# Encoder with a PEER mixer on one core: two more up-projection blocks ahead of the first gate loads, the one-hots of the gate matrix built four steps ahead and gated on GpSimd

## The chip, the core and the metric

One core of one Trainium2 chip runs the whole program as one launch. The metric is the device time of that launch in microseconds (us), lower is better. Three runs of the kernel before took 3058.64 to 3060.64 us, median 3059.3 us.

## What is computed

One encoder layer on 512 tokens of width 2048: windowed attention beside a bidirectional recurrent block, an output projection, and a PEER channel mixer. The change lies in the PEER mixer. Its reference, cut:

```
q = (xt @ w_pq).reshape(T, PEER_HEADS, 2, PEER_HALF)
s1, s2 = einsum(q[:, :, 0], sub_k1), einsum(q[:, :, 1], sub_k2)
v1, i1 = lax.top_k(s1, 16);  v2, i2 = lax.top_k(s2, 16)
cand = v1[..., :, None] + v2[..., None, :]
sc, sel = lax.top_k(cand, 16)          # per head; expert = i1 * 128 + i2
gates = softmax(sc)
act = gelu(einsum('cd,ced->ce', xc, u_emb[expert]))
out = einsum('ce,ced->cd', gates * act, v_emb[expert])
```

There are 16384 experts, 128 of them per token (8 heads of 16).

## The kernel before

Attention, the recurrence, the output projection and the PEER queries fill the first 880 us or so. From there on the program works through the experts.

**Two ways to the experts.** Tokens 0 to 159 gather the rows of their experts from HBM (`gather_gen`): a gather is an indirect DMA that GpSimd (POOL) issues (L1147), and each is followed by one VectorE (DVE) instruction over 2048 elements, a product with the token's row (`gu`, L1154) or a weighted sum (`gv`, L1173). One such pair is a tick. Two gathers are always issued ahead. The other 352 tokens are computed densely: all experts, in 128 blocks of 128, with weights that are zero where a token did not choose an expert.

**The dense part.** An up-projection block (`u_block`) multiplies one block of u_emb with the 352 tokens: 48 matmuls on TensorE (PE), L297 to L299. Its float32 weights are loaded by SyncE (SP, L255) and split into a rounded part `hi` (ScalarE, ACT, L269) and a rest `lo` (DVE, L281). `take` for block b issues the split of block b+1. ACT applies the gelu (L1123, `ga`), and the result stays in SBUF or is spilled to HBM (`ad`).

**The gate matrix.** The weights of the dense tokens form a matrix G (expert by token), made by `g_step`, 4 tokens at a time, in 88 steps. For each token a one-hot row of i1 (`ohA`) and of i2 (`ohB`) is made on DVE (L1208, two instructions of 512 elements a step). `ohA` is multiplied by the gate: in even steps on DVE (L1214, one instruction), in odd steps on ACT (L1212, four). Four small matmuls (L1234, `ps_G`) make 4 columns of G, ACT copies them to a staging tile (L1219), and after 32 tokens the tile goes to HBM (`gd`, L1221). `g_onehots(n + 3)` is called in step n.

**The order.** `stage_plan` writes the order of this stage by hand before the program is built. It walks through the blocks with assumed costs for PE, DVE and ACT and fills hooks, four in each u block (after every 12 matmuls), with the routing work, the gate steps and the ticks. Blocks with hooks come first (here 37, blocks 0 to 36); three more u blocks follow (37 to 39), and together they are `lead0` = 40. All engines take their instructions in this order.

**The transition.** After block 36 the staging tiles are written out, and SP is asked for G tiles (`load_g`, L1315, waiting for `gd`) and for spilled activations (`reload`, L1310, `gr`). Blocks 37 to 39 each call `beside`, which runs due ticks and `weigh` for 3 expert blocks: DVE multiplies by G (L1321), ACT rounds the product (L1324, `Wh`), DVE takes the rest (L1325, `Wl`). After block 39 the down-projection units (`v_unit`, L1368 to L1370) and the remaining u blocks alternate until about 2960 us.

Of the kernel before, what the change touches and what calls it, by code (L numbers as in the profile page):

```python
# [8 lines left out]
F32 = mybir.dt.float32  # L9
# [3 lines left out]
AF = mybir.ActivationFunctionType  # L13
ALU = mybir.AluOpType
# [28 lines left out]
NB = 4  # L43
G_AHEAD = 3
G_STEPS = [(tt, t) for tt in range(1, NT) for t in range(NB1 if tt == 1 else 0, 128, NB)]

# [11 lines left out]
def stage_plan():  # L58
# [8 lines left out]
    for r in range(6):  # L67
# [3 lines left out]
        if r < 5:  # L71
# [5 lines left out]
                      ("lists", 2)]}.get(r, [])  # L77
    tasks += [("pre", m) for m in range(G_AHEAD)]
    for n in range(len(G_STEPS)):
# [5 lines left out]
    while tasks:  # L85
# [4 lines left out]
        while tasks and max(dve, act) <= pe:  # L90
            if ticks_on and since >= 3.5:
                cur.append(("tick", None))
                dve, since = dve + 2.35, 0.0
                continue
            t = tasks.pop(0)
            if t[0] == "g":
                cost, arg = ((1.37, 2.2, 1.22), (2.06, 0.6, 1.22))[t[1] % 2], t[1]
            elif t[0] == "pre":
                cost, arg = ((2.06, 0.0, 0.0), (1.37, 1.6, 0.0))[t[1] % 2], t[1]
            elif t[0] == "lists":  # L100
                cost, arg = (0.0, 0.5, 0.9), t[1]
            elif t[0] in ("soft_a", "soft_b"):
                cost, arg = (t[2], 0.5, 0.0), t[1]
            else:
                cost, arg = t[1:], None
            cur.append((t[0], arg))
            dve, act, pe = dve + cost[0], act + cost[1], pe + cost[2]
            if t[0] == "prime":
                ticks_on, since = True, -9.0
            if ticks_on:  # L110
                since += cost[0]
            if t[0] in ("tr", "soft_a", "lists"):
                break
# [3 lines left out]
    hooks += [[] for _ in range(4 * nbg - len(hooks))]  # L117
    lead0 = nbg + 3
    done, runs, order = lead0, [], [("u", b) for b in range(lead0)]
# [27 lines left out]
def tile_encoder(  # L147
# [1052 lines left out]
    As, Bs, evac, gst = {}, {}, [], {}  # L1200

    def g_onehots(n):
        tm, ta = G_STEPS[n]
        lt = lts[tm]
        Bs[n] = B = gst["oh"].tile([128, NB, 128], F32, tag="B", name="ohB", bufs=G_AHEAD + 1)
        As[n] = Ao = gst["oh"].tile([128, NB, 128], F32, tag="A", name="ohA", bufs=G_AHEAD + 1)
        for o, j in ((Ao, 0), (B, 1)):
            V.tensor_tensor(o, io_sb.unsqueeze(1).to_broadcast([128, NB, 128]),  # L1208
                            lt[:, j, ta:ta + NB].unsqueeze(2).to_broadcast([128, NB, 128]), op=ALU.is_equal)
        if n % 2:  # L1210
            for t in range(NB):
                A.activation(out=Ao[:, t, :], in_=Ao[:, t, :], func=AF.Copy, scale=lt[:, 2, ta + t:ta + t + 1])  # L1212
        else:
            V.tensor_tensor(Ao, Ao, lt[:, 2, ta:ta + NB].unsqueeze(2).to_broadcast([128, NB, 128]), op=ALU.mult)  # L1214

# [7 lines left out]
    def g_step(n):  # L1223
        flush_evac()
        if n + G_AHEAD < len(G_STEPS):
            g_onehots(n + G_AHEAD)
        tt, ta = G_STEPS[n]
# [54 lines left out]
    psS[:] = [psA, "A"]  # L1282
    for b in range(lead0 - 3):
        hk = iter(hooks[4 * b:4 * b + 4])
# [46 lines left out]

    due = {"now": 0.0, "per": (2 * (NSLOT + NB1) - ticks["n"]) / (2 * NBLK - PR - lead0 + 3)}

# [17 lines left out]

    load_g(0)
    load_g(1)
    for _ in range(3):
        reload()
    for i in range(3):
        u_block(lead0 - 3 + i, beside=lambda: beside(range((0, 3, 6)[i], (3, 6, PR + LEAD)[i])))

# [198 lines left out]
```

## Time and profile before

| what | value |
|---|---|
| median of three runs | 3059.3 us (3058.64 to 3060.64) |
| the profiled execution | 3060.12 us, its span 3058.3 us |
| PE busy in the span | 2933.6 us (96%), clock 0.986 of full |
| DVE busy | 2272.5 us (74%) |
| ACT busy | 1153.3 us (38%) |
| POOL busy | 846.3 us (28%) |
| gate stage, blocks 15 to 36 | 1014.9 to 1293.8 us |

The span is the profile's stretch from the first to the last instruction; the execution takes 1.8 us more. Busy shares are means over stages: in the stretch from 2000 to 2800 us PE is busy for 799.68 of 800 us, so there it sets the pace, while around the gate stage it waits for other engines. In the timeline an instruction's row gives start, duration, engine, line, operation, output and input tiles, and in brackets the idle time of the engine before it and what ended it.

### The profile page before, as it was taken

The page shows a single profiled execution, that of the slowest core. Times are in us where ns is not written, and L with a number is a line of the kernel's source. Part 1 is how long each engine was busy: PE and PEld are TensorE (multiplying, and loading weights), DVE is VectorE, ACT ScalarE, POOL GpSimd, SP SyncE. Part 2 cuts the span into 40 slices and gives each one's busy share as a digit, 9 for nine tenths or more (in the row PEclk, how much of TensorE's full clock was granted, in tenths as well). Part 3 has the DMA queues.
Part 4 walks back from the last instruction along what each step waited for, and adds up shares of the span by engine and source line. Part 5 has one row for each costly group of instructions (what it writes and reads, how often), then busy time and mean ns, then how long its engine had stood idle before and what let it go on. Part 6 is the DMA issues. An engine that isn't in the chain of part 4 may idle for free. (4 is left out here: it accounts for less than half of the span.)

```text
span 3058.3 us, 41550 instructions
## 1 busy us (share of the span) xinstructions
PE 2933.6 (96%) x16965; PEld 2729.7 (89%) x16965; DVE 2272.5 (74%) x3143; ACT 1153.3 (38%) x1529; POOL 846.3 (28%) x539
## 2 busy tenths in 40 slices
PE   8999989999999989979999999999999999999997
PEld 6777867788889988979999999999999999999996
DVE  5773367444987789857888888888787887888874
ACT  5663244343444455523322232323323233232233
POOL 0000121022545113423323433233232333233312
PEclk9999999999999999989999999999999999999998
DMA  5222220133225777789899998988889898898983
GB/s 228 76 85 87 85 109 29 69 131 121 83 101 194 258 281 291 298 316 338 335 337 358 355 345 332 343 335 336 328 333 338 326 342 339 340 343 322 349 300 114
DMA packets 160623, 766.76 MB, mean 251 GB/s; under 512 B 13744, under 2 KB 72896, under 8 KB 74480
## 3 DMA queue, kind: packets, MB, share of 16 engines
q1 hardware_dynamic: 101712, 378.44, 33.8%
q0 software_dynamic: 48000, 345.73, 29.9%
q10 hardware_dynamic: 10720, 39.93, 3.4%
q8 instruction: 133, 2.18, 0.3%
q14 instruction: 58, 0.48, 0.0%
HBM read 722.42 MB, written 41.63 MB: 250 GB/s over the span
## 5 line engine op out<-in xcount | busy, mean ns | idle before, releaser
L281 DVE TENSOR_TENSOR lo<-raw,hi 128x2048 fp32r<-128x2048 f32 x307 | 708.5, 2308 | 456.2 <-ACT hi L269 454.0
L269 ACT CAST hi<-raw 128x2048 fp32r<-128x2048 f32 x316 | 602.4, 1907 | 764.5 <-PE ps_v L1369 517.1
L297 PE MATMUL ps_u<-H,hi 128*128 128x352 f32 x2048 | 666.8, 326 | 14.9 <-ACT hi L269 14.9
L299 PE MATMUL ps_u<-H,lo 128*128 128x352 f32 x2048 | 662.5, 323 | 14.3 <-DVE lo L281 14.3
L1368 PE MATMUL ps_v<-Wh,hi 128*128 128x352 f32 x2048 | 664.0, 324 | 6.8 <-ACT Wh L1324 6.2
L1370 PE MATMUL ps_v<-Wh,lo 128*128 128x352 f32 x2048 | 663.6, 324 | 7.2 <-DVE lo L281 7.2
L1369 PE MATMUL ps_v<-Wl,hi 128*128 128x352 f32 x2048 | 663.4, 324 | 0.8
L298 PE MATMUL ps_u<-L,hi 128*128 128x352 f32 x2048 | 661.3, 323 | 0.0
L1147 POOL DMA_INDIRECT gu<-in_u_emb_dram,idx x160 | 331.6, 2073 | 691.4 <-DVE x L1173 500.9
L1147 POOL DMA_INDIRECT gv<-in_v_emb_dram,idx x160 | 286.7, 1792 | 658.8 <-DVE gu L1154 466.1
L299 PEld LDWEIGHTS ps_u<-H,lo 128*128 128x128 f32 x2048 | 385.6, 188 | 17.7 <-DVE lo L281 17.7
L297 PEld LDWEIGHTS ps_u<-H,hi 128*128 128x128 f32 x2048 | 385.9, 188 | 15.4 <-ACT hi L269 15.2
L1368 PEld LDWEIGHTS ps_v<-Wh,hi 128*128 128x128 f32 x2048 | 386.7, 189 | 10.8 <-ACT Wh L1324 8.0
L1370 PEld LDWEIGHTS ps_v<-Wh,lo 128*128 128x128 f32 x2048 | 386.4, 189 | 8.3 <-DVE lo L281 8.3
L1369 PEld LDWEIGHTS ps_v<-Wl,hi 128*128 128x128 f32 x2048 | 386.5, 189 | 2.2 <-DVE Wl L1325 2.2
L298 PEld LDWEIGHTS ps_u<-L,hi 128*128 128x128 f32 x2048 | 385.9, 188 | 0.0
L1154 DVE SCALAR_TENSOR_TENSOR gu<-gu,xng 128x2048 f32<-128x2048 f32 x160 | 364.8, 2283 | 4.2 <-DMA gu<-in_u_emb_dram,idx 4.2
L1173 DVE SCALAR_TENSOR_TENSOR x<-gv,w,x 128x2048 f32<-128x2048 f32 x128 | 300.1, 2345 | 2.9 <-DMA gv<-in_v_emb_dram,idx 2.6
L1123 ACT ACTIVATE ga<-ps_u 128x352 f32<-128x352 f32 x128 | 59.1, 462 | 195.3 <-PE ps_u L299 194.3
L1324 ACT CAST Wh<-ga 128x352 fp32r<-128x352 f32 x73 | 35.5, 487 | 223.3 <-DVE ga L1321 223.3
L297 PE MATMUL ps_cm<-xh,hi 128*128 128x512 f32 x256 | 106.0, 414 | 11.5 <-ACT xh L369 9.1
L1234 PE MATMUL ps_G<-ohA,ohB 128*128 128x128 f32 x704 | 92.0, 279 | 25.4 <-ACT stg L1219 17.4
(311 smaller groups left out, 3792.3 us busy)
## 6 DMA issues: line engine op xcount, KB each, us to landing
raw<-in_u_t_dram SPq DMA_DIRECT2D x128, 1024.0 KB, 6.2
raw<-in_v_t_dram SPq DMA_DIRECT2D x128, 1024.0 KB, 9.0
raw<-in_w_dram SPq DMA_DIRECT2D x28, 1024.0 KB, 4.8
gd<-stg ACTq DMA_DIRECT2D x11, 2048.0 KB, 10.1
G<-gd SPq DMA_DIRECT2D x32, 704.0 KB, 11.0
raw<-in_w_out_dram SPq DMA_DIRECT2D x16, 1024.0 KB, 4.7
raw<-in_w_pq_dram SPq DMA_DIRECT2D x16, 1024.0 KB, 5.0
ad<-ga ACTq DMA_DIRECT2D x55, 176.0 KB, 3.5
```

Of the source, the lines that this page charges most:

```text
L269: A.copy(hi, raw)
L281: en.tensor_tensor(lo[:, c], raw[:, c], hi.bitcast(F32)[:, c], op=ALU.subtract)
L297: T.matmul(ps, ah, bh, start=first, stop=False)
L298: T.matmul(ps, ah, bl, start=False, stop=False)
L299: T.matmul(ps, al, bh, start=False, stop=last)
L1147: P.indirect_dma_start(out=g, out_offset=None, in_=u_emb if kind == "u" else v_emb, in_offset=bass.IndirectOffsetOnAxis(ap=ix, axis=0))
L1154: V.scalar_tensor_tensor(out=g, in0=g, scalar=1.0, in1=xs_t["x"], op0=ALU.mult, op1=ALU.mult, accum_out=a_t[h][:, k:k + 1])
L1173: V.scalar_tensor_tensor(out=d, in0=g, scalar=wk, in1=d, op0=ALU.mult, op1=ALU.add)
L1234: T.matmul(ps[:, t, :], B[:, t, :], Ao[:, t, :], start=True, stop=True)
L1368: T.matmul(ps[:, 0:TD], hi[:, cc], Wh, start=j == 0, stop=False)
L1369: T.matmul(ps[:, 0:TD], hi[:, cc], Wl, start=False, stop=False)
L1370: T.matmul(ps[:, 0:TD], lo[:, cc], Wh, start=False, stop=j == PR - 1)
```

## The change

Four things change together.

1. The planner books both kinds of gate step at the same cost and allows a hook to end after an odd step. It now fills 33 blocks with hooks where it filled 37.
2. The multiplication of `ohA` by the gate leaves DVE and ACT and goes to POOL, one instruction of 128x512 for every step (88 in all).
3. `g_onehots` is split: in step n, `ohA` of step n + 4 and `ohB` and the multiplication of step n + 3 are issued. `ohA` has five buffers, `ohB` four.
4. `N_TRANS` = 5 u blocks stand between the last hook block and the first `v_unit`, and the G tiles and spilled activations are requested after the second. So `lead0` is 38, and 52 blocks are spilled where 55 were.

```diff
+N_TRANS = 5
-    tasks += [("pre", m) for m in range(G_AHEAD)]
+    tasks += [("pre", m) for m in range(G_AHEAD + 1)]
...
-                cost, arg = ((1.37, 2.2, 1.22), (2.06, 0.6, 1.22))[t[1] % 2], t[1]
+                cost, arg = (1.37, 0.6, 1.22), t[1]
...
-                cost, arg = ((2.06, 0.0, 0.0), (1.37, 1.6, 0.0))[t[1] % 2], t[1]
+                cost, arg = (1.37, 0.0, 0.0), t[1]
...
-            if t[0] in ("tr", "soft_a", "lists"):
+            if t[0] in ("tr", "soft_a", "lists") or t[0] == "g" and t[1] % 2:
...
-    lead0 = nbg + 3
+    lead0 = nbg + N_TRANS
...
+    def g_one(lt, ta, j):
+        o = gst["oh"].tile([128, NB, 128], F32, tag="AB"[j], name="oh" + "AB"[j], bufs=G_AHEAD + 2 - j)
+        V.tensor_tensor(o, io_sb.unsqueeze(1).to_broadcast([128, NB, 128]),
+                        lt[:, j, ta:ta + NB].unsqueeze(2).to_broadcast([128, NB, 128]), op=ALU.is_equal)
+        return o
     def g_onehots(n):
-        tm, ta = G_STEPS[n]
-        lt = lts[tm]
-        Bs[n] = B = gst["oh"].tile([128, NB, 128], F32, tag="B", name="ohB", bufs=G_AHEAD + 1)
-        As[n] = Ao = gst["oh"].tile([128, NB, 128], F32, tag="A", name="ohA", bufs=G_AHEAD + 1)
-        for o, j in ((Ao, 0), (B, 1)):
-            V.tensor_tensor(o, ..., op=ALU.is_equal)
-        if n % 2:
-            for t in range(NB):
-                A.activation(out=Ao[:, t, :], in_=Ao[:, t, :], func=AF.Copy, scale=lt[:, 2, ta + t:ta + t + 1])
-        else:
-            V.tensor_tensor(Ao, Ao, lt[:, 2, ta:ta + NB].unsqueeze(2).to_broadcast([128, NB, 128]), op=ALU.mult)
+        if n < len(G_STEPS):
+            tm, ta = G_STEPS[n]
+            As[n] = g_one(lts[tm], ta, 0)
+        n -= 1
+        if 0 <= n < len(G_STEPS):
+            tm, ta = G_STEPS[n]
+            Bs[n] = g_one(lts[tm], ta, 1)
+            P.tensor_tensor(As[n], As[n], lts[tm][:, 2, ta:ta + NB].unsqueeze(2).to_broadcast([128, NB, 128]), op=ALU.mult)
...
-        if n + G_AHEAD < len(G_STEPS):
-            g_onehots(n + G_AHEAD)
+        g_onehots(n + G_AHEAD + 1)
...
-    load_g(0)
-    load_g(1)
-    for _ in range(3):
-        reload()
-    for i in range(3):
-        u_block(lead0 - 3 + i, beside=lambda: beside(range((0, 3, 6)[i], (3, 6, PR + LEAD)[i])))
+    for i in range(N_TRANS):
+        u_block(lead0 - N_TRANS + i, beside=lambda: beside(((), (), range(3), range(3, 6), range(6, PR + LEAD))[i]))
+        if i == 1:
+            load_g(0)
+            load_g(1)
+            for _ in range(3):
+                reload()
```

What the planner now writes cannot be read from the diff, so the order is shown at two places.

On DVE, in the middle of the gate stage (the pieces start at a gate step; L1205 of the change is L1208 of before, and L282, L1155, L1174 are its L281, L1154, L1173). Before:

```order
L1208 TENSOR_TENSOR ohA<-io_sb,lt 128x512
L1208 TENSOR_TENSOR ohB<-io_sb,lt 128x512
L1208 TENSOR_TENSOR ohA<-io_sb,lt 128x512
L1208 TENSOR_TENSOR ohB<-io_sb,lt 128x512
L1214 TENSOR_TENSOR ohA<-ohA,lt 128x512
L281 TENSOR_TENSOR lo<-raw,hi 128x2048
L1208 TENSOR_TENSOR ohA<-io_sb,lt 128x512
L1208 TENSOR_TENSOR ohB<-io_sb,lt 128x512
L1154 SCALAR_TENSOR_TENSOR gu,act<-gu,xng 128x2048
```

and in the change, with POOL's own rows of the same stage behind them:

```order
L1174 SCALAR_TENSOR_TENSOR x_0_2586<-gv,w,x_0_2586 128x2048
L282 TENSOR_TENSOR lo<-raw,hi 128x2048
L1205 TENSOR_TENSOR ohA<-io_sb,lt 128x512
L1205 TENSOR_TENSOR ohB<-io_sb,lt 128x512
L1205 TENSOR_TENSOR ohA<-io_sb,lt 128x512
L1205 TENSOR_TENSOR ohB<-io_sb,lt 128x512
L1205 TENSOR_TENSOR ohA<-io_sb,lt 128x512
L1205 TENSOR_TENSOR ohB<-io_sb,lt 128x512
L1155 SCALAR_TENSOR_TENSOR gu,act<-gu,xng 128x2048
```

```order
L1218 TENSOR_TENSOR ohA<-ohA,lt 128x512 x3
L1148 DMA gu<-in_u_emb_dram,idx 128x2048
L1218 TENSOR_TENSOR ohA<-ohA,lt 128x512 x3
L1148 DMA gv<-in_v_emb_dram,idx 128x2048
L1218 TENSOR_TENSOR ohA<-ohA,lt 128x512 x3
```

The multiplications (L1214) are gone from DVE, and stand three by three between the gathers in POOL's queue, where there were gathers alone.

On ACT, at the end of the gate stage (`ga` ends a u block, `hi` is the split of a later block, `gd` the last write of the gate matrix, `Wh` the first weights). Before:

```order
L1123 ACTIVATE ga<-ps_u 128x352
L1125 DMA ad<-ga 128x352
L1219 COPY stg<-ps_G 128x128x4 x2
L1221 DMA gd<-stg 128x4096
L269 CAST hi<-raw 128x2048
L1324 CAST Wh<-gr 128x352 x3
L1123 ACTIVATE ga<-ps_u 128x352
```

and in the change:

```order
L1124 ACTIVATE ga<-ps_u 128x352
L1126 DMA ad<-ga 128x352
L1223 COPY stg<-ps_G 128x128x4 x2
L1225 DMA gd<-stg 128x4096
L270 CAST hi<-raw 128x2048
L1124 ACTIVATE ga<-ps_u 128x352
L1126 DMA ad<-ga 128x352
L270 CAST hi<-raw 128x2048
L1124 ACTIVATE ga<-ps_u 128x352
L1126 DMA ad<-ga 128x352
L270 CAST hi<-raw 128x2048
L1327 CAST Wh<-gr 128x352 x3
```

Between the last write of the gate matrix and the first weights stand three `hi` where there was one.

## Rows read from the trace of the kernel before

**Rows 1.** Busy time of the engines in three stretches: the gate stage, the transition, and the later stage. Columns: stretch, its length, busy us and instructions of each engine, granted clock of PE, busy share of the DMA engines, GB/s.
```profile
1014.90:1293.80 278.90, 253.46 (x1754) 247.30 (x1753) 250.65 (x296) 148.80 (x309) 82.04 (x30) 1.00 0.75 278
1293.80:1349.00 55.20, 35.32 (x196) 33.76 (x195) 28.01 (x30) 17.19 (x22) 10.80 (x5) 0.81 0.84 299
2000.00:2800.00 800.00, 799.68 (x4992) 799.42 (x4992) 648.77 (x539) 240.82 (x207) 251.79 (x142) 1.00 0.90 335
```

**Rows 2.** Timeline of ACT and PE: the gelu of block 14, with which the gate stage begins, that of block 36, with which it ends, and the first matmul of block 39.
```profile
1014.88 0.47 ACT L1123 ACTIVATE ga<-ps_u 128x352 f32<-128x352 f32 x1
...
1293.75 0.47 ACT L1123 ACTIVATE ga<-ps_u 128x352 f32<-128x352 f32 x1 [2.20 <-PE ps_u L299]
...
1323.99 0.66 PE L297 MATMUL ps_u<-H,hi 128*128 128x352 f32 x1 [14.92 <-ACT hi L269]
```

**Rows 3.** What PE waited for in the gate stage, 1014.9 to 1293.8 us: us in total, times, longest.
```profile
PE ps_G L1234 <- ACT stg L1219: 17.4, 15, 2.7
PE ps_G L1234 <- DVE ohB L1208: 4.7, 4, 1.2
PE ps_G L1234 <- DVE ohA L1214: 2.0, 3, 0.7
PE ps_G L1234 <- ACT ohA L1212: 1.1, 1, 1.1
```

**Rows 4.** What PE waited for in the transition, 1293.8 to 1349 us.
```profile
PE ps_u L297 <- ACT hi L269: 14.9, 1, 14.9
PE ps_v L1370 <- DVE lo L281: 3.4, 1, 3.4
PE ps_u L299 <- DVE lo L281: 1.4, 1, 1.4
```

**Rows 5.** Groups of instructions in the gate stage, DVE's and one of ACT's: line, engine, operation, out<-in, shapes, count | busy us, mean ns | idle before them.
```profile
L1208 DVE TENSOR_TENSOR ohA<-io_sb,lt 128x512 f32<-128x512 f32 x88 | 60.0, 682 | 0.0
L281 DVE TENSOR_TENSOR lo<-raw,hi 128x2048 fp32r<-128x2048 f32 x22 | 50.4, 2289 | 30.5 <-ACT hi L269 29.4 <-issue 1.2
L1154 DVE SCALAR_TENSOR_TENSOR gu<-gu,xng 128x2048 f32<-128x2048 f32 x22 | 50.2, 2281 | 0.0
L1214 DVE TENSOR_TENSOR ohA<-ohA,lt 128x512 f32<-128x512 f32 x44 | 30.1, 684 | 0.0
L1212 ACT ACTIVATE ohA<-ohA,lt 128x128 f32<-128x128 f32 x176 | 56.4, 391 | 112.2 <-DVE ohA L1208 112.2
```

**Rows 6.** Timeline of POOL and DVE at 911 to 918 us: two POOL operations of 512 elements and two DVE splits of 2048 that overlap them.
```profile
911.19 1.05 POOL L1041 TENSOR_TENSOR eq<-ab,io_sb 128x512 f32<-128x512 f32 x1
912.20 3.11 POOL L1041 TENSOR_TENSOR eq<-ab,io_sb 128x512 f32<-128x512 f32 x1
...
911.55 2.84 DVE L281 TENSOR_TENSOR lo<-raw,hi 128x2048 fp32r<-128x2048 f32 x1
...
914.31 3.14 DVE L281 TENSOR_TENSOR lo<-raw,hi 128x2048 fp32r<-128x2048 f32 x1
```

**Rows 7.** Timeline of POOL and DVE at 929 to 932 us, a POOL multiplication of 256 elements that waits behind a DVE split, the DVE operation that follows it, and the same DVE operation at 981 us.
```profile
929.11 2.41 POOL L1057 TENSOR_TENSOR eq<-eq,tf 128x256 f32<-128x256 f32 x1 [13.80 <-ACT eq L1055]
...
930.83 0.83 DVE L1016 TENSOR_TENSOR cand<-tv 128x128 f32<-128x128 f32 x1
...
980.85 0.27 DVE L1016 TENSOR_TENSOR cand<-tv 128x128 f32<-128x128 f32 x1
```

**Rows 8.** POOL's multiplications of 512 elements at the end of the run, no operand repeated, as a group, columns as in rows 5.
```profile
L1433 POOL TENSOR_TENSOR o<-o,gf 128x512 f32<-128x512 f32 x8 | 10.1, 1280 | 0.2 <-ACT jk L1432 0.2
```

**Rows 9.** POOL's gathers: the two groups of the gate stage (columns as in rows 5), one gather from the timeline, and five rows of DVE's timeline while it ran.
```profile
L1147 POOL DMA_INDIRECT gu<-in_u_emb_dram,idx x20 | 72.0, 3598 | 164.8 <-DVE gu L1154 99.3 <-DVE x L1173 65.6
L1147 POOL DMA_INDIRECT gv<-in_v_emb_dram,idx x10 | 10.1, 1008 | 38.5 <-DVE gu L1154 36.7 <-issue 1.8
...
1226.45 9.17 POOL L1147 DMA_INDIRECT gu<-in_u_emb_dram,idx  x1 [5.93 <-DVE x L1173]
...
1226.10 2.28 DVE L281 TENSOR_TENSOR lo<-raw,hi 128x2048 fp32r<-128x2048 f32 x1
1228.30 0.68 DVE L1208 TENSOR_TENSOR ohA<-io_sb,lt 128x512 f32<-128x512 f32 x1
1228.90 0.68 DVE L1208 TENSOR_TENSOR ohB<-io_sb,lt 128x512 f32<-128x512 f32 x1
...
1232.52 2.28 DVE L1154 SCALAR_TENSOR_TENSOR gu<-gu,xng 128x2048 f32<-128x2048 f32 x1
1234.73 0.08 DVE L1154 DVE_READ_ACCUMULATOR gu<-gu,xng 128x1 f32 x1
```

**Rows 10.** Timeline of the transition, ACT, SP and DVE: the last write of the gate matrix, the request for the G tiles, the first product with them, and the split that block 39 waits for.
```profile
1295.72 0.33 ACTq L1221 DMA_DIRECT2D gd<-stg  x1
...
1308.99 1.49 SPq L1315 DMA_DIRECT2D G<-gd  x2
...
1317.21 0.53 DVE L1321 TENSOR_TENSOR gr<-gr,G 128x352 f32<-128x352 f32 x1 [16.89 <-DMA gr<-ad]
...
1322.04 1.90 ACT L269 CAST hi<-raw 128x2048 fp32r<-128x2048 f32 x1 [0.40 <-ACT ga L1123]
```

**Rows 11.** Two windows of 10 us behind the wait of the transition, columns as in rows 1.
```profile
1320.00:1330.00 10.00, 4.64 (x14) 4.19 (x15) 8.07 (x11) 3.96 (x6) 2.77 (x1) 0.50 0.50 158
1330.00:1340.00 10.00, 9.95 (x57) 9.65 (x56) 6.63 (x7) 3.48 (x5) 2.75 (x1) 0.91 1.04 388
```

More of the change, by code (lines that the diff above doesn't have):

```diff
@@ L1200, in tile_encoder @@
     As, Bs, evac, gst = {}, {}, [], {}
-    def g_onehots(n):
-        tm, ta = G_STEPS[n]
-        lt = lts[tm]
-        Bs[n] = B = gst["oh"].tile([128, NB, 128], F32, tag="B", name="ohB", bufs=G_AHEAD + 1)
-        As[n] = Ao = gst["oh"].tile([128, NB, 128], F32, tag="A", name="ohA", bufs=G_AHEAD + 1)
-        for o, j in ((Ao, 0), (B, 1)):
-            V.tensor_tensor(o, io_sb.unsqueeze(1).to_broadcast([128, NB, 128]),
-                            lt[:, j, ta:ta + NB].unsqueeze(2).to_broadcast([128, NB, 128]), op=ALU.is_equal)
-        if n % 2:
-            for t in range(NB):
-                A.activation(out=Ao[:, t, :], in_=Ao[:, t, :], func=AF.Copy, scale=lt[:, 2, ta + t:ta + t + 1])
-        else:
-            V.tensor_tensor(Ao, Ao, lt[:, 2, ta:ta + NB].unsqueeze(2).to_broadcast([128, NB, 128]), op=ALU.mult)
+    def g_one(lt, ta, j):
[3 more added lines that the diff above has]
+        return o
+    def g_onehots(n):
+        if n < len(G_STEPS):
[6 more added lines that the diff above has]
+            P.tensor_tensor(As[n], As[n], lts[tm][:, 2, ta:ta + NB].unsqueeze(2).to_broadcast([128, NB, 128]), op=ALU.mult)
     def flush_evac(keep=1):
@@ L1282, in tile_encoder @@
     psS[:] = [psA, "A"]
-    for b in range(lead0 - 3):
+    for b in range(lead0 - N_TRANS):
         hk = iter(hooks[4 * b:4 * b + 4])
@@ L1330, in weigh @@
             reload()
-    due = {"now": 0.0, "per": (2 * (NSLOT + NB1) - ticks["n"]) / (2 * NBLK - PR - lead0 + 3)}
+    due = {"now": 0.0, "per": (2 * (NSLOT + NB1) - ticks["n"]) / (2 * NBLK - PR - lead0 + N_TRANS)}
     late_ev = []
```

## The prediction, made before the change was run

> **What bounds the kernel now.** I read busy time by stretches first, then PE's waits, then the groups of instructions of the stretch that the change touches, and last the timeline at the places where POOL and DVE meet. In the later stage PE is busy for 799.68 of 800 us [rows 1]. Nothing there can be won or lost unless PE's own work changes, and it doesn't: the change moves matmuls, and removes none. So the time moves only with PE's idle time in the gate stage and the transition, and what is won or lost there stays to the end.
>
> The gate stage runs from the gelu of block 14 at 1014.9 us to that of block 36 at 1293.8 us [rows 2]: 278.9 us, 22 blocks and 88 gate steps. PE's waits in it sum to 25.2 us, 17.4 of them for ACT to empty a PSUM bank and 7.8 for one-hots [rows 3]. DVE is busy for 250.65 of 278.9 us [rows 1]: it is the next engine in line. In the transition PE waits 14.9 us in one piece for the split of block 39, and 1.4 and 3.4 us for `lo` [rows 4].
>
> **PE's work in both versions.** Blocks 37 and 38 run without gate work from 1293.75 us to 1323.99 - 14.92 = 1309.07 us [rows 2], so a block costs PE 7.66 us. The 22 blocks of the gate stage cost 168.5 us, the waits 25.2, and what remains of 278.9 is 85.2 us for the gate matmuls, 0.97 us a step. The change does the same 88 steps beside 18 blocks (15 to 32): 137.9 + 85.2 = 223.1 us, if PE never waits.
>
> **DVE's work in the changed gate stage.** It starts from 250.65 us [rows 1]. The 44 multiplications go. Their rows last 684 ns each [rows 5], but such operations start 0.60 us apart (1228.30 to 1228.90 [rows 9]), so 44 x 0.60 = 26.4 us go. Four blocks fewer take four splits of 2.2 us (1226.10 to 1228.30 [rows 9]) out of the stage, 8.8 us; they come later, with their blocks. The planner puts 31 ticks beside these blocks where there were 30, +2.3 us [rows 5]. That leaves 217.8 us of DVE, just under PE's 223.1.
>
> **The multiplications on POOL.** This is the term that decides. While POOL runs an operation with two SBUF inputs, a DVE operation with two SBUF inputs stands still, and the other way round. POOL's first operation starts at 911.19 and lasts 1.05 us; a DVE split that starts 0.36 us into it takes 2.84 us where the usual one takes 2.29 [rows 5, 6]: 0.55 us lost, so the hold lasts 0.91 us. POOL's second operation is issued at 912.20, gets through only when that split is done, and takes 3.11 us; the next split, behind it, takes 3.14 us, 0.85 us over [rows 6]. The two take turns. The one-hots hold POOL off as well: a gather of POOL that starts at 1226.45 lasts 9.17 us, across a split, the gate steps' instructions of 0.60 us from 1228.30 to 1232.52 and a product, and ends just behind the short read at 1234.73 [rows 9]. So all of DVE's 217.8 us excludes a multiplication on POOL, and each of the 88 multiplications stops DVE whenever DVE has work, which it always has here.
>
> What one costs DVE is not in the trace: no POOL operation of before has this shape. The nearest row has the same 512 elements, repeats an operand along the inner axis as the new one does, and cost 0.85 to 0.91 us [rows 6]. Above it lies the multiplication of 512 elements with nothing repeated, 1.28 us [rows 8]. Below it lies a multiplication of 256 elements, half the size, that cost DVE 0.83 - 0.27 = 0.56 us [rows 7]; below nothing it can't cost, since a POOL operation frees no DVE time beyond what I took off already. I take 0.9 us, by the nearest row: 88 x 0.9 = 79.2 us.
>
> The Trainium skill, SBUF — State Buffer, section SBUF: two separate sides, speaks against this change: it calls the ports shared by DVE and GpSimd an exclusive lock that is held for the full instruction. By that the price would be the whole run of 1.05 us and the forecast about 13 us higher; the rows show a hold a little shorter than the run [rows 6].
>
> **Sum for the gate stage.** DVE and POOL together need 217.8 + 79.2 = 297.0 us one after the other, PE 223.1. The stage lasts 297, and PE waits 73.9 us in it, where it waited 25.2: **+48.7 us**. The stall's new face is `ps_G` waiting for POOL's `ohA`, and next to it `ps_u` waiting for `lo`, because DVE comes late to everything in its queue. ACT loses 56.4 us of multiplications [rows 5]; that is worth at most the part of the 17.4 us of PSUM waits that came from ACT's queue, and these are hidden behind DVE now. The gathers stand behind multiplications on POOL, three between two of them. DVE never waits for a gather in the stage today (idle before `gu` 0.0 [rows 5]), and each is issued two ticks ahead of its use, so I cost that at nothing; if the cover is gone, it is the second rival.
>
> **The transition.** In the kernel before, `gd` is written at 1295.72, SP can ask for G at 1308.99, the first product comes at 1317.21, and the split that PE waits for runs from 1322.04 to 1323.94 [rows 10]: 30.2 us after the gelu of block 36. Blocks 37 and 38, whose splits stand ahead of the first `Wh` on ACT, cover 15.3 us of it. In the change three splits stand there, and four blocks are ready: 33 to 36, 30.6 us. The chain itself has no reason to shorten, and SP's extra loads of u blocks in front of the G request end before `gd` has landed (a split of 1.9 and 2.3 us behind one block of 7.66, some 12 us, against 15.2). So the 14.9 and 1.4 us go. With them goes what the slow clock cost: after the long wait PE was granted 0.50 of full speed, the lower of its two levels (1.2 of 2.4 GHz), and did 14 matmuls in 4.64 us and 57 in the next 10 us [rows 11]; at 0.16 us a matmul (7.66 / 48) that is 2.4 + 0.8 = 3.2 us. I leave 2 us of waits (bounds 0 and 8), since ticks stand beside the weights on DVE: 14.9 + 1.4 + 3.2 - 2 = **-17.5 us**. The 3.4 us at the first down-projections [rows 4] stay.
>
> **Edits with no price.** Three spilled blocks fewer, a slightly lower rate of ticks later on, and a fifth `ohA` buffer lie beside a stage in which PE is never idle [rows 1].
>
> **Total.** 48.7 - 17.5 = +31.2 us on the profiled execution's 3060.1 us gives 3091.3; that execution is 0.8 us over the median of the three runs, so **3091 us**, 1% slower.
>
> **Rivals.**
>
> *The gain comes through (faster).* If a multiplication costs DVE little, because it fits into gaps or is shorter than its neighbours, the stage is PE's again. The point from which this decides is 217.8 + 88 x L = 223.1 + 25.2 + 17.5, L = 0.55 us, about what the operation of half the size cost [rows 7]. For it speaks that the new operation repeats one value over 128 elements, where the nearest row repeats over 16. Against it, that the row's 0.85 us would have to shrink by a third. With L near nothing, the 7.8 us for one-hots go, of the 17.4 us none to half, and the transition's 17.5: 3060.1 - 25.3 to 34.0, that is 3026 to 3035 us. Near L = 0.55 the change is worth nothing: 3060.
>
> *POOL's queue.* The 20 gathers `gu` of the stage take 72.0 us [rows 9] where a `gv`, which mostly isn't held, takes 1.0 [rows 9]; 52 us are spent held off by DVE, up to 8.2 at a time. Today nothing stands behind them. Now multiplications do, and PE has none in hand when DVE and POOL set the pace. While a gather is held DVE runs unhindered, so not all of it is lost; with half of it on the path, +26: 3117 us.
>
> *The two blocks don't cover.* If the G tiles land later, or the splits of the new blocks come as late as the weights, the 17.5 us stay: 3108 us. Against it stands the order on ACT, three splits ahead of the first `Wh`.
>
> **How the numbers follow.** What a measurement of this kernel can tell from no change is about 0.2%, 6 us. Chances: the forecast 0.52, POOL's queue 0.10, no cover 0.06, together 0.68 slower; near break-even 0.10; faster 0.22. The forecast's own range is 3065 (a price of 0.6) to 3118 (a price of 1.2). To hold 8 in 10, the range must reach into the faster case: 3034 to 3118 us.
>
> **What would show it.** Right: the gate stage of 18 blocks lasts 285 to 310 us; PE's waits there are 60 to 90 us and name POOL's `ohA` or DVE; POOL's multiplications run about 1.05 us alone and 2 to 3 us behind a DVE operation; DVE's one-hots, at 0.68 us now, show rows of 1.5 us; the wait of 14.9 us is gone. Wrong: one-hot rows stay at 0.68 us with multiplications beside them, or the stage ends within 250 us.

## The result, and the profile after

The changed kernel took 3097.23 us (median, 3095.21 to 3099.98) against 3058.97 us before, a ratio of 1.0126 with a 95% interval of 1.0108 to 1.0143. That is 38 us slower, where 32 were forecast. Times and ratios here and below are of undisturbed executions; two of the eleven of the transition alone, of 3221 and 5775 us, are left out as disturbed. The profiled execution took 3099.98 us, its span 3098.2 us, 39.9 us over that of before.

Busy time in the gate stage (now blocks 15 to 32), in the transition and in the later stage; columns as in [rows 1]:

```profile
1018.40:1322.20 303.80, 249.26 (x1562) 242.23 (x1561) 300.73 (x249) 90.76 (x124) 159.05 (x119) 0.89 0.67 243
1322.20:1380.00 57.80, 48.00 (x274) 46.54 (x274) 33.48 (x33) 17.80 (x23) 12.64 (x7) 0.88 0.91 333
2000.00:2800.00 800.00, 799.98 (x4992) 799.71 (x4991) 642.06 (x530) 243.92 (x214) 234.85 (x139) 1.00 0.89 333
```

DVE is busy for 300.73 of 303.8 us in the gate stage: it sets the pace, at 99% where it had 90% [rows 1]. PE stands idle for 54.5 us and runs at a granted clock of 0.89. The later stage is as before.

What PE waited for in the gate stage, as in [rows 3]:

```profile
PE ps_G L1237 <- DVE ohB L1205: 49.6, 28, 5.0
...
PE ps_G L1237 <- ACT stg L1223: 0.7, 1, 0.7
```

The 17.4 us of waits for ACT's `stg` are 0.7. One large wait is left, for DVE's one-hots.

DVE's groups of that stage, columns as in [rows 5], and then POOL's:

```profile
L1205 DVE TENSOR_TENSOR ohA<-io_sb,lt 128x512 f32<-128x512 f32 x88 | 101.9, 1158 | 0.0
L1155 DVE SCALAR_TENSOR_TENSOR gu<-gu,xng 128x2048 f32<-128x2048 f32 x23 | 72.9, 3168 | 0.0
L1205 DVE TENSOR_TENSOR ohB<-io_sb,lt 128x512 f32<-128x512 f32 x88 | 59.7, 678 | 0.0
L282 DVE TENSOR_TENSOR lo<-raw,hi 128x2048 fp32r<-128x2048 f32 x18 | 53.7, 2986 | 5.4 <-ACT hi L270 5.4
L1174 DVE SCALAR_TENSOR_TENSOR x<-gv,w,x 128x2048 f32<-128x2048 f32 x9 | 30.8, 3424 | 0.0
...
L1218 POOL TENSOR_TENSOR ohA<-ohA,lt 128x512 f32<-128x512 f32 x88 | 116.3, 1322 | 143.3 <-DVE ohA L1205 142.2 <-issue 0.7
L1148 POOL DMA_INDIRECT gu<-in_u_emb_dram,idx x21 | 32.6, 1553 | 6.9 <-DVE x L1174 3.9 <-issue 1.8
L1148 POOL DMA_INDIRECT gv<-in_v_emb_dram,idx x10 | 12.5, 1248 | 3.8 <-DVE gu L1155 2.4 <-issue 0.5
```

The same DVE instructions do the same work and last longer: `ohA` 1158 ns where it had 682, `lo` 2986 for 2289, `gu` 3168 for 2281. `ohB` alone keeps its length: it is issued just behind the `ohA` that took the blow. The timeline shows it, DVE's rows and then POOL's:

```profile
1250.30 0.68 DVE L1205 TENSOR_TENSOR ohA<-io_sb,lt 128x512 f32<-128x512 f32 x1
1250.90 0.68 DVE L1205 TENSOR_TENSOR ohB<-io_sb,lt 128x512 f32<-128x512 f32 x1
1251.50 1.52 DVE L1205 TENSOR_TENSOR ohA<-io_sb,lt 128x512 f32<-128x512 f32 x1
1252.94 0.68 DVE L1205 TENSOR_TENSOR ohB<-io_sb,lt 128x512 f32<-128x512 f32 x1
1253.55 3.56 DVE L1155 SCALAR_TENSOR_TENSOR gu<-gu,xng 128x2048 f32<-128x2048 f32 x1
...
1251.05 1.42 POOL L1218 TENSOR_TENSOR ohA<-ohA,lt 128x512 f32<-128x512 f32 x1 [2.83 <-DVE ohA L1205]
1252.62 1.25 POOL L1148 DMA_INDIRECT gu<-in_u_emb_dram,idx  x1
1253.89 1.05 POOL L1218 TENSOR_TENSOR ohA<-ohA,lt 128x512 f32<-128x512 f32 x1
```

A multiplication that POOL starts at 1251.05 stretches the `ohA` of 1251.50 by 0.84 us (1.52 for 0.68). The next one, at 1253.89, falls with the end of a gather's issue into one product, which loses 1.28 us (3.56 for 2.28).

The slow clock, in two windows of 6.6 us behind the longest wait of the stage (4.99 us, up to 1119.52):

```profile
1116.60:1123.20 6.60, 3.68 (x15) 3.71 (x16) 6.60 (x8) 0.59 (x1) 3.57 (x3) 0.50 0.63 261
1123.40:1130.00 6.60, 6.60 (x48) 6.60 (x48) 6.60 (x7) 3.34 (x4) 3.10 (x4) 1.00 0.57 189
```

In the first window PE waits until 1119.52, is granted 0.50 of its clock (1.2 of 2.4 GHz) and does 15 matmuls; in the second it runs at full clock and does 48.

In the transition these are PE's waits, as in [rows 4], and SP's, ACT's and DVE's rows that answer to [rows 10]:

```profile
PE ps_u L298 <- ACT hi L270: 7.7, 1, 7.7
PE ps_u L300 <- DVE lo L282: 1.4, 1, 1.4
PE ps_v L1374 <- DVE lo L282: 0.5, 1, 0.5
```

```profile
1328.88 6.52 SPq L256 DMA_DIRECT2D raw<-in_u_t_dram  x2
1335.87 9.74 SPq L1318 DMA_DIRECT2D G<-gd  x2
1345.66 4.76 SPq L1313 DMA_DIRECT2D gr<-ad  x3
...
1322.22 0.47 ACT L1124 ACTIVATE ga<-ps_u 128x352 f32<-128x352 f32 x1 [9.41 <-PE ps_u L300]
1324.19 0.33 ACTq L1225 DMA_DIRECT2D gd<-stg  x1
...
1353.87 0.53 DVE L1324 TENSOR_TENSOR gr<-gr,G 128x352 f32<-128x352 f32 x1 [8.81 <-DMA gr<-ad]
...
1358.70 1.90 ACT L270 CAST hi<-raw 128x2048 fp32r<-128x2048 f32 x1 [0.40 <-ACT ga L1124]
```

The wait for the split has gone from 14.9 to 7.7 us, not away. From the gelu that ends the stage to the end of that split it now takes 1322.22 to 1360.60, 38.4 us, where it took 30.2. Of that, the way from the request for G to the first product takes 18.0 us (1335.87 to 1353.87), where it took 8.2 [rows 10]. What that product waits for last is not G but a spilled activation (`gr`), which SP requests behind G: the two requests of G hold SP for 9.74 us, where they held it for 1.49.

### The profile page after: what moved, and what is told of

The parts are those of the page before. It is cut to its first block, busy times and chain, and to the rows that moved or that the text cites. A ratio compares the mean times of both kernels' runs of the same rounds, so it can differ in the third digit from the quotient of the medians.

```text
span 3098.2 us, 41493 instructions
## 1 busy us (share of the span) xinstructions
PE 2958.3 (95%) x16965; PEld 2754.9 (89%) x16965; DVE 2330.4 (75%) x3099; ACT 1105.0 (36%) x1353; POOL 902.6 (29%) x627
## 5 line engine op out<-in xcount | busy, mean ns | idle before, releaser
L282 DVE TENSOR_TENSOR lo<-raw,hi 128x2048 fp32r<-128x2048 f32 x307 | 721.0, 2349 | 452.4 <-ACT hi L270 451.3
L298 PE MATMUL ps_u<-H,hi 128*128 128x352 f32 x2048 | 675.4, 330 | 7.7 <-ACT hi L270 7.7
L300 PE MATMUL ps_u<-H,lo 128*128 128x352 f32 x2048 | 669.3, 327 | 14.0 <-DVE lo L282 14.0
L299 PE MATMUL ps_u<-L,hi 128*128 128x352 f32 x2048 | 668.5, 326 | 0.0
L1148 POOL DMA_INDIRECT gu<-in_u_emb_dram,idx x160 | 278.5, 1740 | 542.1 <-DVE x L1174 440.9
L1155 DVE SCALAR_TENSOR_TENSOR gu<-gu,xng 128x2048 f32<-128x2048 f32 x160 | 385.3, 2410 | 1.3 <-DMA gu<-in_u_emb_dram,idx 1.3
L1174 DVE SCALAR_TENSOR_TENSOR x<-gv,w,x 128x2048 f32<-128x2048 f32 x128 | 309.8, 2420 | 8.8 <-DMA gv<-in_v_emb_dram,idx 8.8
L1218 POOL TENSOR_TENSOR ohA<-ohA,lt 128x512 f32<-128x512 f32 x88 | 116.3, 1322 | 143.3 <-DVE ohA L1205 142.2
L1237 PE MATMUL ps_G<-ohA,ohB 128*128 128x128 f32 x704 | 103.4, 297 | 53.5 <-DVE ohB L1205 49.6
L1237 PEld LDWEIGHTS ps_G<-ohA,ohB 128*128 128x128 f32 x704 | 95.9, 209 | 60.2 <-issue 60.2
```

The source lines that it names most:

```text
L282: en.tensor_tensor(lo[:, c], raw[:, c], hi.bitcast(F32)[:, c], op=ALU.subtract)
L298: T.matmul(ps, ah, bh, start=first, stop=False)
L299: T.matmul(ps, ah, bl, start=False, stop=False)
L300: T.matmul(ps, al, bh, start=False, stop=last)
L1148: P.indirect_dma_start(out=g, out_offset=None, in_=u_emb if kind == "u" else v_emb, in_offset=bass.IndirectOffsetOnAxis(ap=ix, axis=0))
L1155: V.scalar_tensor_tensor(out=g, in0=g, scalar=1.0, in1=xs_t["x"], op0=ALU.mult, op1=ALU.mult, accum_out=a_t[h][:, k:k + 1])
```

## Experiments

Theory A: each multiplication on GpSimd holds DVE for about as long as it runs, DVE sets the gate stage, and so the change loses there. The rivals stand in the expectations. Each ratio is to the kernel before on the same chip. Stages are blocks 15 to 32 unless said otherwise; the table has PE, DVE and ACT in us.

| kernel | ratio to before, 95% | stage | PE idle | DVE | ACT |
|---|---|---|---|---|---|
| the change | 1.0126 (1.0108 to 1.0143) | 303.8 | 54.5 | 300.7 | 90.8 |
| no multiplication (e1) | 0.985 (0.9832 to 0.9867) | 223.0 | 5.1 | 216.2 | 90.1 |
| DVE and ACT in turns (e2) | 0.9941 (0.9925 to 0.9958) | 248.7 | 24.2 | 242.1 | 139.3 |
| half the elements (e6) | 0.9997 (0.9981 to 1.0012) | 266.7 | 31.3 | 263.5 | 90.8 |
| fused on DVE (e7) | 0.9963 (0.9948 to 0.9978) | 257.5 | 31.4 | 254.4 | 90.7 |
| all on ACT (e8) | 0.9936 (0.9913 to 0.9959) | 247.7 | 22.2 | 217.3 | 189.4 |
| one-input one-hots (e11) | 1.0184 (1.0168 to 1.02) | 322.3 | 61.9 | 319.2 | 90.8 |

### The multiplications left out

```diff
-            P.tensor_tensor(As[n], As[n], lts[tm][:, 2, ta:ta + NB].unsqueeze(2).to_broadcast([128, NB, 128]), op=ALU.mult)
```

> The change with the 88 gate multiplications left out altogether, so that G holds ones in place of gates; all else as in the change. Theory A (the multiplications on POOL stop DVE's two-input operations, 84.5 us in the changed trace): without them DVE needs 217.8 us beside 18 blocks, PE 223.1, so the gate stage shrinks from 303.8 to 225 to 240 us, PE waits under 15 us in it, the one-hots ohA are back at 0.68 us, and the time is 3097 - 64 to 79 = 3018 to 3033 us. Theory B (the denser plan of 33 blocks is itself too tight, whatever the gating costs): DVE still comes late, the stage stays over 270 us and the time over 3060 us.

Measured 3015.94 us. Its gate stage, columns as in [rows 1]:

```profile
1019.70:1242.70 223.00, 217.89 (x1562) 216.27 (x1562) 216.22 (x249) 90.05 (x126) 81.59 (x31) 1.00 0.88 331
```

The same 1562 matmuls take PE 217.89 us at full clock, in a stage of 223.0. So the 88 multiplications cost the stage 80.8 us and the run 0.0276 of its time, 84 us; DVE's busy time differs by 84.5 us, 0.96 us a multiplication. The whole loss of the change is theirs, and without them there would be a gain of some 46 us.

### Half of each multiplication

```diff
-            P.tensor_tensor(As[n], As[n], ...[:, 2, ta:ta + NB]..., op=ALU.mult)
+            P.tensor_tensor(As[n][:, 0:2, :], As[n][:, 0:2, :], ...[:, 2, ta:ta + 2]..., op=ALU.mult)
```

> The change with POOL multiplying only the first two of the four tokens of a step (256 elements in place of 512, 88 instructions as before), so that half of G's columns hold ones. Theory A (DVE is stopped for as long as POOL's operation holds the ports, which goes with its size): the price falls from 0.96 to about 0.55 us, DVE needs 217.8 + 88 x 0.55 = 266 us, the stage lasts 262 to 272 us and the time is 3097 - 32 to 42 = 3055 to 3065 us; ohA's rows behind a multiplication last 1.2 us in place of 1.52. Theory B (a fixed price for each POOL instruction, from the hand-over): the stage stays at 295 to 304 us and the time at 3090 us or more.

Measured 3060.94 us. DVE's one-hots and POOL's multiplications in the stage:

```profile
L1205 DVE TENSOR_TENSOR ohA<-io_sb,lt 128x512 f32<-128x512 f32 x88 | 80.7, 917 | 0.0
...
L1218 POOL TENSOR_TENSOR ohA<-ohA,lt 128x256 f32<-128x256 f32 x88 | 78.7, 894 | 143.4 <-DVE ohA L1205 142.2 <-issue 0.7
```

As many instructions and dependences, half the elements: the price falls to (263.5 - 216.2) / 88 = 0.54 us. An `ohA` that a multiplication falls into lasts 1.10 us (the one at 1204.81 us, say; 1.2 were expected), so a single blow is 0.42 us, half of 0.84. The price goes with POOL's running time, not with the number of instructions or their place in a queue.

### Does a DVE operation with one tile as input escape?

```diff
-        V.tensor_tensor(o, io_sb.unsqueeze(1).to_broadcast([128, NB, 128]),
-                        lt[:, j, ta:ta + NB].unsqueeze(2).to_broadcast([128, NB, 128]), op=ALU.is_equal)
+        for t in range(NB):
+            V.tensor_scalar(out=o[:, t, :], in0=io_sb, scalar1=lt[:, j, ta + t:ta + t + 1],
+                            scalar2=None, op0=ALU.is_equal)
```

> The change with both one-hots made by four single-input operations each (128x128, compare io_sb with one value per partition) instead of one operation of two inputs over 128x512; GpSimd multiplies all 512 elements as in the change. Theory A (GpSimd and DVE exclude each other only where both read two SBUF tiles): the new one-hot operations keep their length of about 0.29 us (0.20 apart) while a multiplication runs beside them, only lo, gu and x still show rows 0.8 us longer; DVE needs 217.8 + 88 x (8 x 0.20 - 1.2) = 253 us plus at most 50 multiplications x 0.9 = 45, so the stage lasts 255 to 298 us. Rival (any DVE operation stands still): rows of 1.1 us or more among the one-hots, and the stage lasts 253 + 79 = 332 us or more, time 3120 or more.

Measured 3115.82 us. DVE's timeline (four instructions to a row) and POOL's beside it, and the two groups of one-hots:

```profile
1247.56 0.86 DVE L1206 TENSOR_SCALAR ohA<-io_sb,lt 128x128 f32<-128x128 f32 x4
1248.35 1.65 DVE L1206 TENSOR_SCALAR ohB<-io_sb,lt 128x128 f32<-128x128 f32 x4
1249.91 0.86 DVE L1206 TENSOR_SCALAR ohA<-io_sb,lt 128x128 f32<-128x128 f32 x4
1250.70 1.65 DVE L1206 TENSOR_SCALAR ohB<-io_sb,lt 128x128 f32<-128x128 f32 x4
...
1248.60 1.12 POOL L1219 TENSOR_TENSOR ohA<-ohA,lt 128x512 f32<-128x512 f32 x1 [3.44 <-PE ps_G L1238]
1250.95 1.12 POOL L1219 TENSOR_TENSOR ohA<-ohA,lt 128x512 f32<-128x512 f32 x1 [1.23 <-DVE ohA L1206]
...
L1206 DVE TENSOR_SCALAR ohB<-io_sb,lt 128x128 f32<-128x128 f32 x352 | 147.2, 477 | 0.0
L1206 DVE TENSOR_SCALAR ohA<-io_sb,lt 128x128 f32<-128x128 f32 x352 | 80.0, 286 | 0.0
```

The four comparisons that a multiplication falls into last 1.65 us for 0.86, so 0.79 us are lost; over the stage it is 352 x (0.477 - 0.286) / 88 = 0.76 us each. The condition of theory A that I had put on it (both engines reading two SBUF tiles) is wrong: an operation that reads one tile and one value per partition stands still as well. The rival had the mechanism, though its 332 us were 10 too many. An operation with no second input at all was not tried.

### Multiplications on GpSimd in the kernel before

```diff
-        if n % 2:
-            ... (four activations on ACT)
-        else:
-            V.tensor_tensor(Ao, Ao, ..., op=ALU.mult)
+        P.tensor_tensor(Ao, Ao, lt[:, 2, ta:ta + NB].unsqueeze(2).to_broadcast([128, NB, 128]), op=ALU.mult)
```

> The kernel before with one edit: all 88 multiplications on POOL, plan and transition as before (37 blocks with hooks, three more). Theory A: DVE gives up 26.4 us and is stopped for 88 x 0.96 = 84.5 us, 250.65 - 26.4 + 84.5 = 308.8 us; the gate stage goes from 278.9 to 305 to 312 us and the time to 3059 + 26 to 35 = 3085 to 3094 us. Theory B: taking work off DVE and ACT helps the looser plan: the stage falls under 270 us and the time under 3055 us.

Measured 3081.63 us, ratio 1.0071 (1.0054 to 1.0088): slower, but by 22 us only. Blocks 15 to 36 lasted 300.1 us with DVE busy for 294.5. Over 250.65 - 26.4 = 224.2 us without multiplications on DVE that is 0.80 us each. The direction holds, the size was expected too high.

### Other places for the multiplication

On DVE in even steps and on ACT in odd ones, as before, with all else of the change:

```diff
-            P.tensor_tensor(As[n], As[n], ..., op=ALU.mult)
+            if n % 2:
+                for t in range(NB):
+                    A.activation(out=As[n][:, t, :], in_=As[n][:, t, :], func=AF.Copy, scale=lts[tm][:, 2, ta + t:ta + t + 1])
+            else:
+                V.tensor_tensor(As[n], As[n], ..., op=ALU.mult)
```

> The change with the gating taken back from POOL: even steps on DVE (one instruction), odd steps on ACT (four), as before; plan, four steps ahead and transition as in the change. Theory A: DVE needs 217.8 + 44 x 0.60 = 244.2 us for the 18 blocks and is not stopped by POOL; the stage lasts 244 to 260 us, the time is 3097 - 44 to 60 = 3037 to 3053 us, faster than before. Theory B: the stage stays near 300 us and the time over 3080 us.

Measured 3042.46 us: the rest of the change is worth about 18 us. DVE sets the stage again, at 242.1 of 248.7 us. With the four blocks that now follow it (30.6 us) the stage is no shorter than before, 279.3 for 278.9 us, so the gain lies behind it. Next, all on ACT (the four activations in every step):

> The change with all 88 gatings on ACT (four instructions each), none on POOL or DVE. Theory A: DVE needs 217.8 us as without gating; ACT goes from 90.8 to about 90.8 + 88 x 1.2 = 196 us of some 225; the stage lasts 225 to 240 us and the time is 3018 to 3033 us. Rival: ACT gets late for the emptying of PSUM, PE waits for stg and hi, the stage lasts over 248 us and the time is over 3042 us, no better than with the gating split between DVE and ACT.

Measured 3041.23 us, within 1 us of the rival's bounds (248 and 3042) and far from theory A, but not by the rival's waits: PE hardly waits for `stg`, and waits for `hi` come to DVE. DVE needs 217.3 us and yet the stage lasts 247.7, as its waits tell, PE's and then DVE's:

```profile
PE ps_G L1238 <- DVE ohB L1205: 19.1, 14, 4.2
PE ps_G L1238 <- ACT stg L1224: 2.8, 3, 1.3
...
DVE lo L282 <- ACT hi L270: 31.0, 16, 5.4
```

DVE now idles 31.0 us behind ACT's `hi`, which stands behind the activations in ACT's queue, and the one-hots behind `lo` come late to PE. The multiplication fused into the comparison:

```diff
+            for t in range(NB):
+                V.tensor_scalar(out=As[n][:, t, :], in0=io_sb, scalar1=lts[tm][:, 0, ta + t:ta + t + 1],
+                                scalar2=lts[tm][:, 2, ta + t:ta + t + 1], op0=ALU.is_equal, op1=ALU.mult)
```

> The change with ohA and its gating made in one go on DVE: for each token one tensor_scalar of 128 elements (equal to i1, times the gate), four a step, nothing on POOL. Operations of this shape start 0.2 us apart in the trace of before, so a step costs 0.6 + 0.8 us on DVE; theory A: 217.8 + 88 x 0.2 = 235.4 us, the stage lasts 235 to 248 us and the time is 3028 to 3041 us. Rival: with two scalars read per partition they cost 0.29 us each one after the other, 217.8 + 88 x 0.56 = 267 us, and the time is over 3055 us.

Measured 3050.0 us, between the two. The 352 instructions last 354 ns each, where the comparison alone, with one value, has 286 ns. DVE's busy time rises from 216.2 to 254.4 us over the kernel without multiplications, 0.43 us a step. A fused step thus costs 0.60 + 0.43 = 1.03 us, little less than a comparison and a multiplication of 512 elements one after the other (2 x 0.60).

### The transition alone

The kernel before with `N_TRANS` = 5, the loop of the change and its loads after the second block, and nothing else:

> The kernel before with one edit: five blocks in the transition, the G tiles requested after the second; gating and hooks as before (37 blocks with hooks, 42 in all ahead of the down-projection). Theory A (two more blocks cover the G chain but for what more loads and gathers cost it on the DMA engines): PE's wait of 14.9 us falls to 5 to 9 us and the slow clock after it gets shorter, so 3059 - 7 to 12 = 3047 to 3052 us. Theory C (as I predicted: the chain stays at 30.2 us and is covered): the wait is under 2 us, 3059 - 17.5 = 3041 us. Theory D (the wait only moves): 3056 to 3062 us.

Median 3055.77 us, ratio 0.9981 (0.9968 to 0.9995), some 6 us won. The trace is of a second run:

> The kernel before with the transition of the change alone, a second look at its trace, since its first one was of a disturbed execution. Theory A (four blocks cover 30.7 us, and the chain is longer than the 30.2 us of before because G and the spilled activations share the DMA engines with loads of u blocks): a wait of 5 to 9 us at the split behind the weights instead of 14.9, the transfer of G 13 us or more from its request to the first product where it took 8.2. Rival (the longer chain comes from the gate stage's new end, with GpSimd's gathers standing behind multiplications): the wait is under 3 us and the chain about 30 us.

It took 3055.67 us, a single run. PE's waits in its transition:

```profile
PE ps_u L298 <- ACT hi L270: 7.5, 1, 7.5
PE ps_u L300 <- DVE lo L282: 3.6, 1, 3.6
PE ps_v L1370 <- ACT Wh L1325: 1.4, 1, 1.4
```

and SP's rows with the split that is waited for:

```profile
1300.27 7.49 SPq L256 DMA_DIRECT2D raw<-in_u_t_dram  x2
1312.40 4.73 SPq L1316 DMA_DIRECT2D G<-gd  x2
...
1330.19 1.90 ACT L270 CAST hi<-raw 128x2048 fp32r<-128x2048 f32 x1 [0.40 <-ACT ga L1124]
```

From the gelu at 1293.67 to the end of the split at 1332.09 it takes 38.4 us, as in the change. No multiplication runs on POOL here, so the longer chain comes from the transition's own edit. Two loads of u blocks stand ahead of G on SP, where in the kernel before SP had none in that stretch, and they move their data beside `gd`, G and `gr`. The delay sits elsewhere on the chain, though: `gd` lands 16.7 us after it is issued (13.1 before, 11.6 in the change), the two requests of G hold SP for 4.73 us (1.49 and 9.74), and the second tile of G lands 12.5 us after the first request (17.5 in the change).

The wait came out as theory A had it, the time just under theory D's. From the end of the gate stage to the end of the program this kernel takes 3053.9 - 1293.7 = 1760.2 us, where the kernel before takes 3058.3 - 1293.8 = 1764.5: so part of what the split's wait gives is lost again behind it.

### The gathers beside the transition left away, and a sixth block

First, the kernel with DVE and ACT in turns, without ticks in the first two blocks of the transition (the later ticks come at a slightly higher rate):

```diff
-    due = {... / (2 * NBLK - PR - lead0 + N_TRANS)}
+    due = {... / (2 * NBLK - PR - lead0 + N_TRANS - 2)}
...
-        u_block(..., beside=lambda: beside(((), (), range(3), range(3, 6), range(6, PR + LEAD))[i]))
+        u_block(..., beside=lambda: beside(((), (), range(3), range(3, 6), range(6, PR + LEAD))[i], i > 1))
```

> The kernel with the gating split between DVE and ACT again (plan, four steps ahead and five blocks as in the change), and no gathers beside the first two of the five transition blocks. In the changed trace the chain from the G request to the first product lasts 18.0 us where it was 8.2. Theory A (gathers of 1 MB issued beside the two new blocks share the DMA engines with G): the wait of 7.6 us falls to 1 to 4 us and the time by 4 to 7 us, to 3035 to 3039 us on the same chip. Theory B (the loads of the u blocks do it, which stay): the wait stays at 6.5 to 8 us, the time within 3 us of 3042.

Ratio 0.9952 (0.9935 to 0.997), no better than 0.9941. The wait at the split falls from 7.6 to 5.0 us, between the two theories, and one of 3.4 us at the first down-projections replaces others of 2.0 us. Then one more block of cover, in that same kernel and in the change:

```diff
-N_TRANS = 5
+N_TRANS = 6
...
-        u_block(..., beside=lambda: beside(((), (), range(3), range(3, 6), range(6, PR + LEAD))[i]))
+        u_block(..., beside=lambda: beside(((), (), (), range(3), range(3, 6), range(6, PR + LEAD))[i]))
```

> Gating back on DVE and ACT as before, and six u blocks instead of five between the last hook block and the first down-projection (no weights beside the first three; G asked after the second as in the change). Theory A (after the gate stage PE only lacks one block of cover: the chain from the last gate matrix write to the first split behind the weights lasts about 38 us, four blocks cover 30.7 us): five blocks cover 38.3 us, the wait of 7.6 us shrinks to under 1.5 us, and with it 1 to 2 us of slow clock; ratio 0.991 (0.990 to 0.9925) where the same kernel with five blocks had 0.9941. Rival (what is taken from this wait comes back at the next one, as without the gathers): the wait at the first split goes, one of 4 us or more stands at the first down-projections, and the ratio stays at 0.9935 to 0.995.

> The change as it is, with six u blocks instead of five in the transition. Theory A: the gate stage stays at 302 to 305 us, the wait of 7.75 us goes, ratio 1.0095 (1.008 to 1.011) where the change had 1.0126. Rival (the wait comes back later): 1.012 to 1.014.

Ratios 0.9959 (0.9945 to 0.9972) and 1.0138 (1.0122 to 1.0154), where five blocks had 0.9941 and 1.0126: theory A's expectation of a gain fell twice, and the first ratio is even above the rival's range. PE's waits in the transition of the first:

```profile
PE ps_u L300 <- DVE lo L282: 4.8, 2, 4.0
PE ps_u L298 <- ACT hi L270: 3.2, 1, 3.2
PE ps_v L1376 <- ACT Wh L1331: 1.8, 2, 1.5
PE ps_v L1378 <- DVE lo L282: 1.2, 1, 1.2
```

The split's wait is 3.2 us where it was 7.6, and the `lo` behind it now costs 4.8 where it cost 2.7. From 1400 to 2000 us PE idles 11.6 us where it idled 7.3. So the cover is paid back with later waits, though not at the first down-projections, where the rival had put them, and which of the transfers sets the transition's length is not settled.

Of the versions that still do all of the multiplications, the fastest are the one with the multiplication back on DVE and ACT, at 0.9941, and the one with all of it on ACT, at 0.9936; their intervals overlap.

## Why the prediction came out as it did

**The deciding term held.** The price of a multiplication was taken as 0.9 us, between 0.56 and 1.28. Measured were 0.96 us in the change and 0.80 in the kernel before. Single blows are 0.84 us, near the 0.85 to 0.91 of [rows 6]; what lifts the mean in the change is that a gather's issue and a multiplication can fall on one instruction together (1.28 us). The 0.96 is DVE's busy time of 300.7 us, where 297.0 was forecast, less 216.2, over 88; the stage is 3 us longer than that. The break-even at 0.55 us came out as well, with half the elements at 0.54 us and a ratio of 0.9997, but in part by luck, since the gains beside it lay elsewhere than I had them (below). The Trainium skill, SBUF — State Buffer, section SBUF: two separate sides, has a lock held for the full instruction. By the 1.05 us of a multiplication that runs freely it would have cost 92 us; DVE lost 84.5, gathers included, so the rows keep the lock and shorten the hold.

**Its condition was wrong.** I had the two engines exclude each other where both read two SBUF tiles. The comparisons with one tile lose 0.76 us too. The sum did not depend on it, since nearly all of DVE's work in the stage has two.

**PE's wait had another name and size.** I named POOL's `ohA` first; the trace names DVE's `ohB`, which is issued behind the slowed `ohA`. PE's waits were 54.5 us instead of 73.9, because I forgot the slow clock inside the stage: with waits of 3 to 5 us strewn through it, the granted clock is 0.89, and the matmuls that take 217.89 us at full clock take 249.26. These 31 us cost no time: DVE was the pace, and a slower PE only waits less.

**POOL's queue** did not become a bound. A gather `gu` takes 1.55 us in the change where it took 3.60 [rows 9], and the longest lasts 2.85 us where one lasted 9.17. POOL is busy for 159 of the stage's 303.8 us.

**The transition is the step that failed in size.** I wrote that the chain had no reason to shorten, kept it at 30.2 us, and let four blocks cover it with 2 us of waits left. The cover came, to 1352.90, but the chain grew to 38.4 us. G's way took 8.2 us before, with the DMA engines at a share of 0.84 (1309.0 to 1317.2 us), and 18.0 us in the change, with the engines at 1.06 (1335.8 to 1353.9): the two added blocks need their own weights, and these are loaded just when G and `gr` must come. Of the 18.0 us, SP is held for 9.7 by the two requests of G (1.5 before), and 8.2 pass from the request for `gr` to the product (6.7 before). That the loads are the cause is argued from their times; only the gathers were taken away in a run, and they were worth 2.6 us of the wait. I had looked only at whether they delay the request on SP, not at whether they share the engines. Waits of 14.9 and 1.4 us and 3.2 us of slow clock became 7.7, 1.4 and 3.4 (8.3 us at a clock of 0.50, 6.89 of them busy, half of that lost). That is -7.0 us instead of -17.5.

**"Edits with no price" was wrong behind the transition, and by about as much as the transition fell short.** Between 1345 and 2000 us PE idled 17.9 us before, and 11.9 after the change's transition ended at 1373 us, as these windows show, of before and of the change:

```profile
1345.00:2000.00 655.00, 637.11 (x3912) 631.67 (x3911) 531.42 (x461) 197.94 (x182) 219.95 (x113) 0.99 0.92 343
```

```profile
1373.00:2000.00 627.00, 615.13 (x3806) 611.57 (x3805) 511.08 (x447) 193.14 (x178) 205.31 (x107) 1.00 0.92 345
```

I had carried the reading of 2000 to 2800 us over to a stretch that has waits of its own, worth -6.0 us here. The slow clock behind such waits comes on top: in these windows a matmul takes 637.11 / 3912 = 0.1629 us before and 615.13 / 3806 = 0.1616 in the change, some 5 us over the stretch.

The whole of it shows in the time from the end of the gate stage to the end of the program, less the 30.6 us of the four blocks that the new plan puts there: 1764.5 us before, 3098.2 - 1322.2 - 30.6 = 1745.4 in the change, so -19.1 us. The other kernels tell which edit that goes with. Where the plan and the five-block transition are both as in the change, and the gathers stay, it is 1742.5 to 1745.4 us wherever the multiplication runs; without the gathers beside its first two blocks it is 1750.9; with six blocks 1748.4 and 1750.2; with the transition alone 1760.2, with neither 1764.9. So some 15 of the 19 us come only with the plan of 33 blocks, which leaves 38 u blocks ahead of the down-projection and 52 spilled, where the transition alone has 42 and 58. The plan without the transition was not run, and which of these counts matters is open.

**The sum.** The stage with its four blocks behind it came to 303.8 + 30.6 - 278.9 = +55.5 us (forecast +48.7), the transition to -7.0 (forecast -17.5), all behind it to -12.1 (forecast 0). The stage also began 3.5 us later, at 1018.4 us for 1014.9; in the runs above it begins anywhere from 1012.6 to 1019.7, so this needs no cause in the change. Together that is the 39.9 us between the spans. The sign and the mechanism were right. The small distance in the total (38 for 32) is in good part luck: the stage and the transition came out 17.3 us worse than forecast, and 12.1 us came back from edits that I had given no price.

## What to carry to other kernels

Before work moves from DVE to GpSimd, look in the trace for a place where the two overlap and read what the DVE instruction gained in length: that, times the count, comes back on DVE, and where DVE has no idle time it lengthens the stage in full. Removing the same work from the path (as in e1) shows first what the move can win at best. When blocks are put in front of a wait as cover, count what these blocks themselves load in the time in which the awaited transfer must come, and look for the next wait behind the one that is covered: the time from there to the end of the program shows what is really won.

## What the runs showed of the hardware

A multiplication on GpSimd stops DVE for less time than it runs: 0.84 us of 1.05 at 512 elements, and 0.42 of 0.63 at 256. It stops DVE also in operations that read one tile and one value per partition (0.79 us a blow). A comparison fused with a multiplication, with two values per partition, is slower than the comparison alone: 354 ns instead of 286 at 128x128. An indirect gather's issue took 2.6 to 3.2 us on average before, with no multiplication and with DVE and ACT in turns, and 1.2 to 1.5 us in the change, fused on DVE and all on ACT; with multiplications on GpSimd in the order of before it took 2.8 us, so they alone don't set it, and what does is open.
